# Order of the routing work ahead of the experts' blocks, and how the first block's input is scaled

## The chip, the cores and the metric

The kernel runs on one core of a Trainium2 chip. The metric is the device time of one execution in microseconds, as a median of several runs. The engines of the core are PE (TensorE), DVE (VectorE), ACT (ScalarE), POOL (GpSimd) and SP (SyncE, which issues the DMAs of the weights here). Each engine works off its own instructions in the order in which they stand, and waits at semaphores for the others.

## What is computed

Two transformer blocks over 256 tokens of 1024 channels, all in float32. The change touches the last step of the second block alone, a mixture of 16 experts in 4 groups:

```python
def hier_moe(h, w_rg, b_rg, w_re, b_re, w1, w3, w2):
    t = h.reshape(-1, d)
    lg = (t @ w_rg + b_rg).astype(jnp.float32)
    g_sel = jnp.argmax(lg, axis=-1)
    w_grp = jnp.take_along_axis(jax.nn.softmax(lg, axis=-1), g_sel[:, None], axis=-1)
    le = (t @ w_re + b_re).astype(jnp.float32).reshape(-1, N_GROUPS, EXPERTS_PER_GROUP)
    le_g = jnp.take_along_axis(le, g_sel[:, None, None], axis=1)[:, 0]
    top_v, top_i = lax.top_k(le_g, TOP_K_IN_GROUP)
    w_top = jax.nn.softmax(top_v, axis=-1) * w_grp
    ...
        y = (jax.nn.silu(t @ w1e) * (t @ w3e)) @ w2e
        return acc + ge[:, None] * y, None
```

`h` is the RMS-normed stream, times (1 + scale), plus a shift. The result is gated, added to the stream and normed once more.

## The kernel before

Ahead of the experts, `merge2` makes the stream `h` (tile `res`) in 8 slices of 128 channels. Beside each slice PE also makes the router's logits (L1371) and transposes the slice to token rows (L1376, tiles `xh`, `xl`), and `sumsq` gathers the squares for the norm: ACT squares, DVE or POOL add four slices up, and PE sums them over the channels after the fourth and the eighth slice (L343).

`moe` then runs: `tokens` starts the output's accumulators with the stream (L1733), `route` makes the routing, and 13 blocks of 64 slots follow. A slot is a place for one token. Experts 12 to 15 have a block each (blocks 0 to 3). The other twelve are sorted by how many tokens they have; the fullest get two blocks, the emptiest share one. So the weights of the experts from block 4 on can be loaded only when the sorted order (`order`, tile `idi`) is known: SP reads the twelve numbers one by one (L1753) and issues the DMAs with them. Weights come as tiles of 1 MB (`ew`), six for an expert, 96 in all, into 19 slots of memory. SP's instructions have one order, so a DMA stands behind the reads that are ahead of it.

`route` is a Python generator: each `next(route)` emits one part of it. Before, part one ends with `rk`, the rank of each token in its expert (L1444); part two makes the gates (the softmaxes, L1452 to L1473); part three makes the experts' order, then per expert the ranks and gates in that order, then the list of extra blocks `eji` for experts that overflow (`moe_rest`, normally none).

For a block, `onehots` makes a matrix `Q` from ranks to slots, `norms` and `rows` gather the slots' token rows with it (PE L1586, L1627; ACT scales them into `xs`), `modulated_slots` transposes them into one bank (PE L1641), and DVE multiplies by `a2` and adds the shift over all 8 slices at once (L1644, L1645; tile `xX`). `per_slot` makes the transposed matrix `xPT` and the slots' gates `gs` (PE L1598, L1612). Then `expert_in` (PE L1674) makes both products into `gu`, `expert_act` makes `xa` (ACT tanh, two instructions of DVE: L1683, L1684), `expert_mid` transposes it (L1692, `xaT`), `expert_out` multiplies by the last weight (L1706), DVE and ACT scale and split it (`xY`), and `expert_add` adds it to the accumulators (L1721). The blocks are staggered: out and add of a block run beside the next ones' input.

The order on each engine is set by the tile framework's scheduler, which places instructions by its own timeline; priorities follow the order of the source, and in the changed kernel `issue_after` keeps an instruction behind another.

Of the kernel before, what the change touches and what calls it, by code (L numbers as in the profile page):

```python
# [15 lines left out]
OP = mybir.AluOpType  # L16
# [161 lines left out]
class Build:  # L178
# [118 lines left out]
    def slab(self, name, n):  # L297
# [33 lines left out]
    def sumsq(self, st, x, tiles, k, eng=None, alone=KT):  # L331

        nc = self.nc
        sq = self.R([128, x.shape[1]], "nt")
        nc.scalar.activation(sq, x, AF.Square)
        if k % 4 and k < alone:
            (eng or nc.gpsimd).tensor_tensor(self.sq, self.sq, sq, op=OP.add)
        else:
            self.sq = sq
        if k % 4 == 3 or k >= alone - 1:  # L340
            for i in reversed(range(len(tiles))):
                t0, n = tiles[i]
                nc.tensor.matmul(st[:n, i:i + 1], self.sq[:, t0:t0 + n], self.ones[:, 0:1], start=False,  # L343
                                 stop=k == KT - 1 and i == 0)

    def rstd(self, st, nt, dim, eps):
# [3 lines left out]
        r = self.R([128, 4], "rr")  # L350
        nc.gpsimd.tensor_tensor(r[:, :nt], v[:, :nt], self.mhalf[:, 0:1].to_broadcast([128, nt]), op=OP.pow)
        return r
# [994 lines left out]
    def merge2(self):  # L1347
# [17 lines left out]
        for k in range(KT):  # L1365
# [30 lines left out]
    def route(self):  # L1396
# [18 lines left out]
        def onehot(name, x):  # L1415
# [28 lines left out]
        ranked = nc.vector.scalar_tensor_tensor(self.rk, pc[:, 0:32].rearrange("p (i e) -> p i e", i=2), 1000.0,  # L1444
                                                sel, op0=OP.add, op1=OP.mult)
        self.ranked = ranked.ins
# [31 lines left out]
        tt(F, pn[:, 0:16][:, None, :].to_broadcast([128, 3, 16]), cr, OP.is_gt)  # L1478
        Ff = F.rearrange("p r e -> p (r e)")
# [25 lines left out]
    def order(self, cnt):  # L1505
# [8 lines left out]
        nc.vector.scalar_tensor_tensor(key, cnt, 16.0, self.C("pri12"), op0=OP.mult, op1=OP.add)  # L1514
        t, M = self.R([128, 12, 12], "mx7"), self.R([128, 12, 12], "mx8")
        tt(t, across(key), down(key), OP.is_gt)
# [4 lines left out]
        self.ids = self.T([128, 12], "idi", I32)  # L1521
        nc.vector.tensor_copy(self.ids, ids)
        rgs = self.small([128, 2, 2, 12], "rgs")
        for a in range(2):
# [47 lines left out]
    def equal(self, rk, w):  # L1572
        m = rk.shape[2]
        Q = self.R([128, 2, m * w], "xQ", dt=F32R)
        self.nc.vector.tensor_tensor(Q.rearrange("p i (a s) -> p i a s", a=m),
                                     self.C("iota")[:, None, None, :w].to_broadcast([128, 2, m, w]),
                                     rk[:, :, :, None].to_broadcast([128, 2, m, w]), op=OP.is_equal)
        return Q

    def norms(self, Q):  # L1580

        nc = self.nc
        m = Q.shape[2]
        ps = self.P("r")
        for i in range(2):
# [48 lines left out]

    def modulated_slots(self, xs, b):

# [5 lines left out]
        X = self.R([128, KT, 64], "xX")  # L1642
        wide = lambda x: x[:, :, None].to_broadcast([128, KT, 64])
        nc.vector.tensor_tensor(X, bank, wide(self.a2), op=OP.mult)  # L1644
        nc.vector.tensor_tensor(X, X, wide(self.mod[:, 24:32, 0]), op=OP.add)  # L1645
        return X
# [17 lines left out]
    def expert_in(self, ws, X):  # L1664
# [5 lines left out]
        for k in range(KT):  # L1670
            for b, w in enumerate(ws):
                for j in range(2):
                    p = 64 * j + m * b
                    nc.tensor.matmul(gu[p:p + m], X[:, k, m * b:m * b + m], w[k // 2][:, k % 2, j], start=k == 0,  # L1674
                                     stop=k == KT - 1)
        return gu
# [47 lines left out]
    def tokens(self):  # L1724
# [4 lines left out]
        self.acc = [self.P(t) for t in "gggr"]  # L1729
        for i in range(2):  # L1730
            for j in range(2):
                for x in (self.xh, self.xl):
                    nc.tensor.matmul(self.acc[2 * i + j], idr, x[:, i, j * 512:(j + 1) * 512], start=x is self.xh,  # L1733
                                     stop=False)

    def moe(self):
# [7 lines left out]
        Q = self.onehots(0)  # L1744
        xs = self.rows(Q, self.norms(Q))
        X = self.modulated_slots(xs, 0)
        a = Ys = PT1 = None
        ids, wins, wouts = {}, {}, {}
        for e in range(N + 1):
# [6 lines left out]
            if e == 0:  # L1756
                next(route)
            if e < N:
                PT, g = self.per_slot(Q, e % 2, self.gate_cols(e))
                if e % 2 and e + 1 < N:  # L1760
                    Q = self.onehots(e + 1)
                    xs = self.rows(Q, self.norms(Q))
                if e == 0:
                    X1 = self.modulated_slots(xs, 1)
                gu = self.expert_in([wins[x] for x in self.BLOCKS[e]], X)
                if e == 0:
                    X = X1
            before = a
# [8 lines left out]
            if e == 0:  # L1777
                next(route)
            if e:
# [130 lines left out]
```

## Time and profile before

| what | us |
|---|---|
| median of 3 runs | 1182.49 (1181.82 to 1184.79) |
| the profiled execution | 1179.23 |
| its span, first to last instruction | 1177.4 |
| PE busy | 1130.7 (96% of the span) |
| DVE busy | 717.7 (61%) |
| ACT busy | 521.8 (44%) |
| the stage from the end of `merge2` to the last instruction | about 937 to 1177 |

A page of a profile tells of one execution. Times in rows are microseconds from the first instruction. A row of a timeline is start, duration, engine, line, operation, output<-inputs, form, and count; in brackets stands how long the engine was idle before it and whose result ended that. A float32 matmul shows as two records. In a list of waits stand the waiting engine and line, whom it waited for, and us in total, times, longest. The lines are those of the kernel before; in the changed kernel L1586 is L1609, L1627 is L1650, L1644 is L1668, L1674 is L1701.

### The profile page before, as it was taken

The page shows a single profiled execution, that of the slowest core. Times are in us where ns is not written, and L with a number is a line of the kernel's source. Part 1 is how long each engine was busy: PE and PEld are TensorE (multiplying, and loading weights), DVE is VectorE, ACT ScalarE, POOL GpSimd, SP SyncE. Part 2 cuts the span into 40 slices and gives each one's busy share as a digit, 9 for nine tenths or more (in the row PEclk, how much of TensorE's full clock was granted, in tenths as well). Part 3 has the DMA queues.
Part 4 walks back from the last instruction along what each step waited for, and adds up shares of the span by engine and source line. Part 5 has one row for each costly group of instructions (what it writes and reads, how often), then busy time and mean ns, then how long its engine had stood idle before and what let it go on. Part 6 is the DMA issues. An engine that isn't in the chain of part 4 may idle for free. (4 is left out here: it accounts for less than half of the span.)

```text
span 1177.4 us, 21644 instructions
## 1 busy us (share of the span) xinstructions
PE 1130.7 (96%) x8718; PEld 946.6 (80%) x8718; DVE 717.7 (61%) x1341; ACT 521.8 (44%) x1068; POOL 274.9 (23%) x299
## 2 busy tenths in 40 slices
PE   6999899999999998999999999999999989999995
PEld 6888799799998998999999999988999844433331
DVE  6868964966555588998445654777556554322333
ACT  6556563344543564545444443566543312212222
POOL 3341237101222236615230156011003100000000
PEclk9999999799999998999999999999999999999998
DMA  6433333132576565897545444312757769999993
GB/s 233 147 140 109 108 108 108 37 112 105 207 265 250 181 235 211 319 362 274 207 177 180 146 144 168 121 70 80 288 183 275 287 233 421 412 421 422 421 421 123
DMA packets 37574, 256.42 MB, mean 218 GB/s; under 512 B 4064, under 2 KB 5600, under 8 KB 7136
## 3 DMA queue, kind: packets, MB, share of 16 engines
q1 hardware_dynamic: 35280, 250.85, 56.7%
q10 hardware_dynamic: 2192, 4.17, 1.1%
q8 instruction: 69, 1.13, 0.4%
q14 instruction: 33, 0.27, 0.1%
HBM read 253.96 MB, written 1.05 MB: 217 GB/s over the span
## 5 line engine op out<-in xcount | busy, mean ns | idle before, releaser
L319 DVE TENSOR_TENSOR w<-raw,w 128x1024 fp32r<-128x1024 f32 (+1 forms) x233 | 296.3, 1282 | 146.6 <-ACT w L318 137.2
L318 ACT ACTIVATE w<-raw 128x1024 fp32r<-128x1024 f32 (+1 forms) x233 | 242.9, 1054 | 236.1 <-PE d L314 142.2
L311 PE MATMUL d<-xh,w 128*128 128x256 f32 (+3 forms) x520 | 138.8, 300 | 1.1 <-ACT xh L318 1.1
L312 PE MATMUL d<-xh,w 128*128 128x256 f32 (+3 forms) x520 | 135.5, 293 | 0.0
L311 PEld LDWEIGHTS d<-xh,w 128*128 128x128 f32 (+1 forms) x520 | 100.3, 193 | 7.3 <-issue 2.9
L1674 PE MATMUL d<-ew,xX 128*64 128x512 f32 (+1 forms) x544 | 102.5, 598 | 0.1
L312 PEld LDWEIGHTS d<-xh,w 128*128 128x128 f32 (+1 forms) x520 | 100.3, 193 | 2.5 <-issue 1.6
L314 PE MATMUL d<-xl,w 128*128 128x256 f32 (+3 forms) x520 | 82.5, 292 | 0.0
L311 PE MATMUL d<-lxh,w 128*128 128x256 f32 x288 | 75.3, 297 | 0.9 <-ACT vc L1211 0.9
L312 PE MATMUL d<-lxh,w 128*128 128x256 f32 x288 | 71.5, 284 | 0.0
L314 PEld LDWEIGHTS d<-xl,w 128*128 128x128 f32 (+1 forms) x520 | 69.5, 188 | 2.1 <-issue 1.1
L1674 PEld LDWEIGHTS d<-ew,xX 128*64 128x64 f32 (+1 forms) x544 | 29.7, 124 | 49.3 <-issue 45.4
L311 PE MATMUL d<-n2h,w 128*128 128x256 f32 x256 | 63.9, 286 | 0.8 <-ACT ur L1054 0.8
L312 PE MATMUL d<-n2h,w 128*128 128x256 f32 x256 | 63.1, 284 | 0.0
L311 PEld LDWEIGHTS d<-lxh,w 128*128 128x128 f32 x288 | 54.8, 190 | 2.9 <-issue 1.3
L1132 DVE SCALAR_TENSOR_TENSOR E<-wmod,sc,E 128x512 f32<-128x512 f32 x56 | 54.5, 974 | 3.0 <-ACT E L1130 1.6
L312 PEld LDWEIGHTS d<-lxh,w 128*128 128x128 f32 x288 | 54.9, 191 | 0.8 <-issue 0.3
L1824 POOL TENSOR_TENSOR fst<-fst,mhalf 128x1 f32<-128x1 f32 x2 | 1.1, 540 | 233.1 <-DVE fst L1823 233.1
L1706 PE MATMUL d<-ew,xaT 128*64 128x512 f32 (+1 forms) x272 | 52.9, 599 | 0.0
L311 PEld LDWEIGHTS d<-n2h,w 128*128 128x128 f32 x256 | 49.0, 191 | 2.2 <-ACT ur L1054 1.2
L1056 POOL TENSOR_TENSOR uu<-ur 128x256 f32<-128x256 f32 x32 | 35.0, 1092 | 61.5 <-ACT ur L1054 61.5
L312 PEld LDWEIGHTS d<-n2h,w 128*128 128x128 f32 x256 | 49.0, 192 | 0.3 <-DVE E L1132 0.2
(552 smaller groups left out, 2709.8 us busy)
## 6 DMA issues: line engine op xcount, KB each, us to landing
ew<-we_in SPq DMA_DIRECT2D x96, 1024.0 KB, 12.1
raw<-w_in SPq DMA_DIRECT2D x62, 1024.0 KB, 4.9
wmod<-wmod_in SPq DMA_DIRECT2D x24, 1024.0 KB, 6.7
raw<-wup_in SPq DMA_DIRECT2D x16, 1024.0 KB, 5.1
raw<-wdn_in SPq DMA_DIRECT2D x16, 1024.0 KB, 5.0
raw<-wao_in SPq DMA_DIRECT2D x8, 1024.0 KB, 5.0
raw<-wbg_in SPq DMA_DIRECT2D x4, 1024.0 KB, 4.9
raw<-wbd_in SPq DMA_DIRECT2D x4, 1024.0 KB, 6.0
```

The costliest lines, as they stand in the source:

```text
L311: nc.tensor.matmul(ps, wh[:, k, :m], xh[:, k, ts], start=first and k == 0, stop=False)
L312: nc.tensor.matmul(ps, wl[:, k, :m], xh[:, k, ts], start=False, stop=False)
L314: nc.tensor.matmul(ps, wh[:, k, :m], xl[:, k, ts], start=False, stop=last and k == kts - 1)
L318: nc.scalar.activation(h, src, AF.Copy)
L319: (eng or nc.gpsimd).tensor_tensor(l, src, h.bitcast(F32), op=OP.subtract)
L1056: nc.gpsimd.tensor_tensor(u, r, r, op=OP.mult)
L1132: nc.vector.scalar_tensor_tensor(t, w(k), sc[:, 2 * k:2 * k + 1], t, op0=OP.mult, op1=OP.add)
L1674: nc.tensor.matmul(gu[p:p + m], X[:, k, m * b:m * b + m], w[k // 2][:, k % 2, j], start=k == 0, stop=k == KT - 1)
L1706: nc.tensor.matmul(y[p:p + m], aT[:, c, m * b:m * b + m], w[c // 2][:, c % 2, j * 512:(j + 1) * 512], start=c == 0, stop=c == 3)
L1824: nc.gpsimd.tensor_tensor(st[:, 3:4], st[:, 2:3], self.mhalf, op=OP.pow)
```

## The change

Five edits, all around the routing.

- `sumsq` in `merge2` gets `alone=6`: the sixth, seventh and eighth slices are summed by PE each as they come, and DVE's additions for the last two go. `rstd` writes to its place at once, without a copy.
- In `route` the two products of the ranks over a column block become one, and three matmuls of ones by ones (`busy`) stand ahead of them, two more ahead of `norms`. Their results are overwritten.
- The experts' order is made directly behind the ranks, from a copy of the counts (`cnt`). Gates, and ranks and gates in the new order (`ordered`), stand behind the first block's input; the extra blocks are made beside block 4.
- Block 0's input is scaled and shifted in halves: four slices by DVE, four by ACT.
- The transposed matrix and gates of block 0 and the input of block 1 stand behind the third step of block 0's `expert_in`.

```diff
+    def busy(self, ps, n, after):
+        with self.tc.issue_after(after):
+            for _ in range(n):
+                self.nc.tensor.matmul(ps[:, :128], self.ones, self.ones, start=True, stop=True)
...
-            self.sumsq(st, h, self.REAL, k, nc.vector if k > 3 else nc.gpsimd)
+            self.sumsq(st, h, self.REAL, k, nc.vector if k > 3 else nc.gpsimd, alone=6)
...
-        nc.vector.tensor_copy(r, self.rstd(self.tot, 2, D, EPS)[:, :2])
+        self.rstd(self.tot, 2, D, EPS, r)
...
-        nc.tensor.matmul(pc[:, 0:16], C("trius"), sel[:, 0], start=True, stop=True)
-        nc.tensor.matmul(pc[:, 16:32], C("trius"), sel[:, 1], start=True, stop=False)
+        self.busy(pc, 3, self.begun)
+        nc.tensor.matmul(pc[:, 0:32], C("trius"), sel.rearrange("p i e -> p (i e)"), start=True, stop=False)
         nc.tensor.matmul(pc[:, 16:32], self.ones, sel[:, 0], start=False, stop=True)
...
-        nc.tensor.matmul(pn[:, 0:16], self.ones, sel[:, 1], start=False, stop=True)
+        self.ranking = nc.tensor.matmul(pn[:, 0:16], self.ones, sel[:, 1], start=False, stop=True).ins
+        cnt = R([128, 16], "cnt")
+        nc.vector.tensor_copy(cnt, pn[:, 0:16])
+        self.order(cnt[:, 0:12])
+        yield
...
-        cap = self.order(pn[:, 0:12])
+        cap = self.ordered()
+        yield
...
+        n = KT // 2 if halves else KT
+        wide = lambda x: x[:, :n, None].to_broadcast([128, n, 64])
+        nc.vector.tensor_tensor(X[:, :n], bank[:, :n], wide(self.a2), op=OP.mult)
+        ins = nc.vector.tensor_tensor(X[:, :n], X[:, :n], wide(self.mod[:, 24:32, 0]), op=OP.add)
+        self.shifted = ins.ins
+        for k in range(n, KT):
+            nc.scalar.activation(X[:, k], bank[:, k], AF.Identity, bias=self.sh2(k), scale=self.a2[:, k:k + 1])
...
-        xs = self.rows(Q, self.norms(Q))
-        X = self.modulated_slots(xs, 0)
+        with self.tc.issue_after(self.placed):
+            next(route)
+        xs = self.rows(Q, self.norms(Q, 2))
+        X = self.modulated_slots(xs, 0, True)
+        shifted = self.shifted
...
             if e == 0:
-                next(route)
-            if e < N:
+                gu = self.expert_in([wins[x] for x in self.BLOCKS[e]], X)
+                with self.tc.issue_after(shifted):
+                    with self.tc.issue_after(self.third):
+                        next(route)
+                        PT, g = self.per_slot(Q, 0, self.gate_cols(0))
+                        X = self.modulated_slots(xs, 1)
...
             if e == 0:
-                next(route)
+                with self.tc.issue_after(shifted):
+                    next(route)
+            if e == 4:
+                with self.tc.issue_after(self.shifted):
+                    next(route)
```

How the order moves, at three places. PE, from the last matmul of `tokens` to the first gathered row (`tabs` holds the triangle of ones, `small` the routing's little tiles), before:

```order
L1733 MATMUL r<-xl,idr 128x512
L1441 MATMUL d<-small,tabs_8673 128x16
L1442 MATMUL d<-small,tabs_8673 128x16
L1443 MATMUL d<-small,ones 128x16
L1586 MATMUL r<-small,xQ 128x1 x2
L1627 MATMUL r<-xh,xQ 128x512
```

and after:

```order
L1763 MATMUL r<-xl,idr 128x512
L309 MATMUL d<-ones 128x128 x3
L1449 MATMUL d<-small,tabs_8673 128x32
L1450 MATMUL d<-small,ones 128x16
L1456 MATMUL r<-small,ones 128x16
L1457 MATMUL r<-small,ones 128x16
L309 MATMUL r<-ones 128x128 x2
L1609 MATMUL r<-small,xQ 128x1 x2
L1650 MATMUL r<-xh,xQ 128x512
```

Three products of the ranks became two, and the counts (L1456, L1457; before they stood behind the transposes of block 0's input) and five matmuls of ones came in.

DVE, from the ranks to block 0's input, before (the last row is the first step of `order`'s comparisons):

```order
L1444 SCALAR_TENSOR_TENSOR small<-d,small 128x32
L1575 TENSOR_TENSOR xQ<-tabs_8673,small 128x256 x2
L1588 COPY ns<-r 128x1
L1644 TENSOR_TENSOR xX<-r,a_3943 128x512
L1514 SCALAR_TENSOR_TENSOR small<-r,tabs_8673 128x12
L1645 TENSOR_TENSOR xX<-xX,mod 128x512
L1615 COPY gs<-r 64x1
L1644 TENSOR_TENSOR xX<-r,a_3943 128x512
L1508 TENSOR_TENSOR mx_10931<-small 128x144
```

and after:

```order
L1451 SCALAR_TENSOR_TENSOR small<-d,small 128x32
L1595 TENSOR_TENSOR xQ<-tabs_8673,small 128x256 x2
L1459 COPY small<-r 128x16
L1525 SCALAR_TENSOR_TENSOR small<-small,tabs_8673 128x12
L1611 COPY ns<-r 128x1
L1519 TENSOR_TENSOR mx_10831<-small 128x144
L1520 TENSOR_REDUCE small<-mx_10831 128x12
L1519 TENSOR_TENSOR small<-small,tabs_8673 128x144
L1519 TENSOR_TENSOR mx_10831<-small,tabs_8673 128x144
L1520 TENSOR_REDUCE small<-mx_10831 128x12
L1533 CAST idi<-small 128x12
L1668 TENSOR_TENSOR xX<-r,a_3943 128x256
```

The whole of `order`, down to the numbers that SP reads, moved from behind block 1's input to ahead of block 0's.

DVE beside the step from block 0 to block 1 (the first row scales block 1's input, `xa` is block 0's activation), before:

```order
L1644 TENSOR_TENSOR xX<-r,a_3943 128x512
L1508 TENSOR_TENSOR mx_10931<-small 128x144
L1683 SCALAR_TENSOR_TENSOR xa<-xa,d 64x512
L1645 TENSOR_TENSOR xX<-xX,mod 128x512
L1509 TENSOR_REDUCE small<-mx_10931 128x12
```

and after:

```order
L1668 TENSOR_TENSOR xX<-r,a_3943 128x512
L1539 TENSOR_TENSOR mx_10949<-small 128x144 x2
L1539 TENSOR_TENSOR mx_10953<-small 128x144 x2
L1638 COPY gs<-r 64x1
L1712 SCALAR_TENSOR_TENSOR xa<-xa,d 64x512
L1669 TENSOR_TENSOR xX<-xX,mod 128x512
L1540 TENSOR_REDUCE small<-mx_10949 128x24
```

Four multiplications of 128x144 and a copy now stand between the two halves of block 1's input, where one multiplication stood.

## Rows read from the trace of the kernel before

**Rows 1.** Busy time by stretch: PE, PEld, DVE, ACT, POOL, clock, DMA share, GB/s.
```profile
980.00:1020.00 40.00, 39.46 (x244) 17.35 (x242) 12.03 (x22) 7.54 (x16) 0.00 (x0) 1.00 1.01 415
```
**Rows 2.** What PE waited for from 980 us on: total us, times, longest.
```profile
PE g L1721 <- DVE xY L1714: 5.7, 5, 2.2
PE r L1692 <- DVE xa L1684: 3.7, 4, 1.2
```
**Rows 3.** Timeline of SP: the last issue of a weight tile.
```profile
1134.78 0.33 SPq L1660 DMA_DIRECT2D ew<-we_in  x1
```
**Rows 4.** DMAs of the weight tiles from 880 us on: issue to landing.
```profile
DMA to landing us min/median/max: 4.9/14.1/20.2
```
**Rows 5.** The view of Rows 1 in 5 us steps around the ranks.
```profile
940.00:945.00 5.00, 2.31 (x15) 1.72 (x14) 4.10 (x27) 0.79 (x3) 0.00 (x0) 1.00 1.00 415
945.00:950.00 5.00, 5.00 (x21) 3.50 (x21) 0.66 (x2) 1.68 (x4) 0.00 (x0) 0.66 0.34 144
```
**Rows 6.** Timeline of PE, from the last sum of squares to block 0.
```profile
937.26 0.50 PE L343 MATMUL r<-ones,nt 128*128 128x1 f32 x4
...
942.84 0.39 PE L1441 MATMUL d<-small,tabs 128*128 128x16 f32 x2 [1.86 <-DVE small L1401]
...
944.51 0.58 PE L1586 MATMUL r<-small,xQ 128*128 128x1 f32 x4 [0.83 <-DVE xQ L1575]
...
945.27 0.39 PE L1627 MATMUL r<-xl,xQ 128*128 128x512 f32 x1
945.50 0.56 PE L1627 MATMUL r<-xh,xQ 128*128 128x512 f32 x1
...
948.13 1.34 PE L1641 MATMUL r<-identm,xs 64*128 64x64 f32 x8
...
950.97 6.22 PE L1674 MATMUL d<-ew,xX 128*64 128x512 f32 x26
```
**Rows 7.** Timeline of DVE over the same stretch.
```profile
935.85 0.41 DVE L1380 TENSOR_TENSOR xl<-g,xh 128x256 fp32r<-128x256 f32 x1
...
938.79 0.17 DVE L1407 COPY small<-rr 128x2 f32<-128x2 f32 x1 [0.82 <-POOL rr L351]
...
940.62 0.16 DVE L1405 TENSOR_REDUCE small<-small 128x2 f32<-128x8 f32 x1 [0.31 <-ACT small L1460]
...
949.50 0.69 DVE L1644 TENSOR_TENSOR xX<-r,a 128x512 f32<-128x512 f32 x1 [4.21 <-PE r L1641]
...
950.23 0.69 DVE L1645 TENSOR_TENSOR xX<-xX,mod 128x512 f32<-128x512 f32 x1
```
**Rows 8.** Timeline of ACT ahead of block 0: a large and a small tile.
```profile
936.90 0.38 ACT L1379 ACTIVATE xh<-g 128x256 fp32r<-128x256 f32 x1 [0.27 <-PE g L1376]
...
940.38 0.20 ACT L1460 ACTIVATE small<-small 128x8 f32<-128x8 f32 x1
```
**Rows 9.** Timeline of PE, from the end of block 0 to block 2.
```profile
961.80 6.23 PE L1674 MATMUL d<-ew,xX 128*64 128x512 f32 x28
...
971.25 0.50 PE L1627 MATMUL r<-xh,xQ 128*128 128x512 f32 x1 [0.64 <-DVE ns L1588]
...
973.43 0.71 PE L1641 MATMUL r<-identm,xs 64*128 64x64 f32 x8 [0.60 <-ACT xs L1631]
...
978.48 6.22 PE L1674 MATMUL d<-ew,xX 128*64 128x512 f32 x26
```
**Rows 10.** Timeline of DVE beside blocks 0 and 1.
```profile
959.65 0.69 DVE L1644 TENSOR_TENSOR xX<-r,a 128x512 f32<-128x512 f32 x1 [2.02 <-PE r L1641]
...
960.47 0.67 DVE L1683 SCALAR_TENSOR_TENSOR xa<-xa,d 64x512 f32<-64x512 f32 x1
961.07 0.68 DVE L1645 TENSOR_TENSOR xX<-xX,mod 128x512 f32<-128x512 f32 x1
...
963.96 0.52 DVE L1508 TENSOR_TENSOR mx<-small,mx 128x144 f32<-128x144 f32 x2
```
**Rows 11.** Timeline of PE near the end: the add of the last block but one.
```profile
1159.77 1.22 PE L1721 MATMUL g<-xY,xPT 128*128 128x512 f32 x3 [1.25 <-DVE xY L1714]
```

More of the change, by code (lines that the diff above doesn't have):

```diff
@@ L342, in sumsq, with rstd @@
                 t0, n = tiles[i]
-                nc.tensor.matmul(st[:n, i:i + 1], self.sq[:, t0:t0 + n], self.ones[:, 0:1], start=False,
-                                 stop=k == KT - 1 and i == 0)
-    def rstd(self, st, nt, dim, eps):
+                ins = nc.tensor.matmul(st[:n, i:i + 1], self.sq[:, t0:t0 + n], self.ones[:, 0:1], start=False,
+                                       stop=k == KT - 1 and i == 0)
+            self.summed = ins.ins
+    def rstd(self, st, nt, dim, eps, r=None):
         nc = self.nc
@@ L349, in rstd @@
         nc.vector.tensor_scalar(v[:, :nt], st[:, :nt], 1.0 / dim, eps, op0=OP.mult, op1=OP.add)
-        r = self.R([128, 4], "rr")
+        r = self.R([128, 4], "rr") if r is None else r
         nc.gpsimd.tensor_tensor(r[:, :nt], v[:, :nt], self.mhalf[:, 0:1].to_broadcast([128, nt]), op=OP.pow)
@@ L1440, in route @@
         pc = self.P("d")
-        nc.tensor.matmul(pc[:, 0:16], C("trius"), sel[:, 0], start=True, stop=True)
-        nc.tensor.matmul(pc[:, 16:32], C("trius"), sel[:, 1], start=True, stop=False)
+        self.busy(pc, 3, self.begun)
+        nc.tensor.matmul(pc[:, 0:32], C("trius"), sel.rearrange("p i e -> p (i e)"), start=True, stop=False)
         nc.tensor.matmul(pc[:, 16:32], self.ones, sel[:, 0], start=False, stop=True)
-        ranked = nc.vector.scalar_tensor_tensor(self.rk, pc[:, 0:32].rearrange("p (i e) -> p i e", i=2), 1000.0,
-                                                sel, op0=OP.add, op1=OP.mult)
-        self.ranked = ranked.ins
+        nc.vector.scalar_tensor_tensor(self.rk, pc[:, 0:32].rearrange("p (i e) -> p i e", i=2), 1000.0,
+                                       sel, op0=OP.add, op1=OP.mult)
         self.r2 = r
@@ L1474, in route @@
         yield
-        cap = self.order(pn[:, 0:12])
+        cap = self.ordered()
+        yield
         F, cr = R([128, 3, 16], "Fc"), self.small([128, 3, 16], "cr3")
         tt(cr, C("r64").rearrange("p (r e) -> p r e", r=3), cap[:, None, :].to_broadcast([128, 3, 16]), OP.add)
-        tt(F, pn[:, 0:16][:, None, :].to_broadcast([128, 3, 16]), cr, OP.is_gt)
+        tt(F, cnt[:, None, :].to_broadcast([128, 3, 16]), cr, OP.is_gt)
         Ff = F.rearrange("p r e -> p (r e)")
@@ L1514, in order @@
         nc.vector.scalar_tensor_tensor(key, cnt, 16.0, self.C("pri12"), op0=OP.mult, op1=OP.add)
-        t, M = self.R([128, 12, 12], "mx7"), self.R([128, 12, 12], "mx8")
+        t, M = self.R([128, 12, 12], "mx7"), self.small([128, 12, 12], "mof")
         tt(t, across(key), down(key), OP.is_gt)
@@ L1522, in order, with ordered @@
         nc.vector.tensor_copy(self.ids, ids)
+        self.place, self.mof = place, M
+    def ordered(self):
+        nc = self.nc
+        tt = lambda o, a, b, op: nc.vector.tensor_tensor(o, a, b, op=op)
+        red = lambda o, a: nc.vector.tensor_reduce(o, a, axis=AX.X, op=OP.add)
+        across = lambda x: x[:, None, :].to_broadcast([128, 12, 12])
+        place, M = self.place, self.mof
         rgs = self.small([128, 2, 2, 12], "rgs")
@@ L1574, in equal, with norms @@
         Q = self.R([128, 2, m * w], "xQ", dt=F32R)
-        self.nc.vector.tensor_tensor(Q.rearrange("p i (a s) -> p i a s", a=m),
-                                     self.C("iota")[:, None, None, :w].to_broadcast([128, 2, m, w]),
-                                     rk[:, :, :, None].to_broadcast([128, 2, m, w]), op=OP.is_equal)
+        ins = self.nc.vector.tensor_tensor(Q.rearrange("p i (a s) -> p i a s", a=m),
+                                           self.C("iota")[:, None, None, :w].to_broadcast([128, 2, m, w]),
+                                           rk[:, :, :, None].to_broadcast([128, 2, m, w]), op=OP.is_equal)
+        self.placed = ins.ins
         return Q
-    def norms(self, Q):
+    def norms(self, Q, busy=0):
         nc = self.nc
@@ L1584, in norms @@
         ps = self.P("r")
+        if busy:
+            self.busy(ps, busy, self.ranking)
         for i in range(2):
@@ L1633, in rows, with modulated_slots @@
         return xs
-    def modulated_slots(self, xs, b):
+    def modulated_slots(self, xs, b, halves=False):
         nc = self.nc
@@ L1642, in modulated_slots @@
         X = self.R([128, KT, 64], "xX")
-        wide = lambda x: x[:, :, None].to_broadcast([128, KT, 64])
-        nc.vector.tensor_tensor(X, bank, wide(self.a2), op=OP.mult)
-        nc.vector.tensor_tensor(X, X, wide(self.mod[:, 24:32, 0]), op=OP.add)
+        n = KT // 2 if halves else KT
[5 more added lines that the diff above has]
+            nc.scalar.activation(X[:, k], bank[:, k], AF.Identity, bias=self.sh2(k), scale=self.a2[:, k:k + 1])
         return X
@@ L1673, in expert_in @@
                     p = 64 * j + m * b
-                    nc.tensor.matmul(gu[p:p + m], X[:, k, m * b:m * b + m], w[k // 2][:, k % 2, j], start=k == 0,
-                                     stop=k == KT - 1)
+                    ins = nc.tensor.matmul(gu[p:p + m], X[:, k, m * b:m * b + m], w[k // 2][:, k % 2, j],
+                                           start=k == 0, stop=k == KT - 1)
+                    if k == 2:
+                        self.third = ins.ins
         return gu
@@ L1729, in tokens @@
         self.acc = [self.P(t) for t in "gggr"]
[L1730 to L1734, printed above, removed]
+        with self.tc.issue_after(self.summed):
+            for i in range(2):
+                for j in range(2):
+                    for x in (self.xh, self.xl):
+                        ins = nc.tensor.matmul(self.acc[2 * i + j], idr, x[:, i, j * 512:(j + 1) * 512],
+                                               start=x is self.xh, stop=False)
+        self.begun = ins.ins
     def moe(self):
@@ L1756, in moe @@
             if e == 0:
-                next(route)
-            if e < N:
+                gu = self.expert_in([wins[x] for x in self.BLOCKS[e]], X)
[4 more added lines that the diff above has]
+                        X = self.modulated_slots(xs, 1)
+            elif e < N:
                 PT, g = self.per_slot(Q, e % 2, self.gate_cols(e))
```

4 lines of the change are left out of this document (removed).

## Prediction

> **What bounds the kernel now.** I read the view by stretch first, for the expert blocks. Between 980 and 1020 us PE is busy for 39.46 of 40.00 us at clock 1.00 [rows 1]; the DMA engines are as full there, at a share of 1.01, so the second question is whether PE ever waits for a weight. It doesn't: the two largest entries in the list of its waits from 980 us on are the adds waiting for `xY` (5.7 us in 5 waits) and the transposes waiting for `xa` (3.7 in 4), both for DVE [rows 2]. The last weight tile is issued at 1134.78 [rows 3], and no tile took more than 20.2 us to land [rows 4], so it is there by about 1155.0; PE reaches the add of the last block but one at 1159.77 [rows 11], and only then the rest of the last products. Weights have some 5 us in hand at the tightest place. From this two things follow. Earlier weights are worth nothing by themselves; and if PE starts a block earlier by less than about 5 us, the end comes earlier by as much. So the question is how early blocks 0, 1 and 2 start.
>
> The timelines of PE and DVE between 935 and 980 us answer it. There PE is not full: 2.31 of 5 us from 940 to 945 [rows 5]. It waits 1.86 us for DVE's chain to the ranks and 0.83 for `xQ` [rows 6], then its granted clock is 0.66 on the mean of the next 5 us [rows 5], that is, part of these at the lower level.
>
> **The change part by part.** All sums are made against the profiled execution, 1179.23 us with a span of 1177.4 (1.8 lie around it); the median of the runs, 1182.49, is 3.3 us longer, and I take the difference over unchanged.
>
> Sums of squares. Two more groups of channel sums come to a full PE. Four records took 0.50 us [rows 6], and their spacing is less, so each group costs between 0.2 and 0.5; I take 0.36, together −0.72. In exchange DVE loses an addition of four slices; the nearest row is an operation of 128x256 at 0.41 [rows 7], and with the order of `xh` and `xl` behind it I take 0.55 back. The copy that goes (0.17 [rows 7]) comes on top. Net about 0, bounds −0.5 to +0.5.
>
> Gates out of the chain to the ranks. In it DVE waits 0.31 us for ACT's exponential at 940.62 [rows 7]; that wait and a small instruction go: +0.35. The product of ranks in one goes from three pairs of records to two: at most 0.39, the duration of such a pair [rows 6]; I take 0.23, the spacing of two records, from 945.27 to 945.50 [rows 6]. The counts and the matmuls of ones stand in time in which PE waited (1.86 and 0.83 [rows 6]), so they cost nothing unless they last longer than that: three before the ranks and, behind them, two counts and two of ones, each of these below 0.39 by the counts' kin in [rows 6], some 0.9 us together against about 1 us in which DVE makes `rk` and `xQ`. At worst +0.2 of delay.
>
> The clock. Two gathers with the same shape follow each other by 0.23 us at 945.27 [rows 6]; from 945.50 six of them take until 948.13, 2.63 us, where 6 x 0.23 makes 1.4. Ahead of the fall stood the two waits of PE. With the five matmuls of ones and the counts in them most of that idle time is filled, and I let the fall go: +1.2. The bounds are 0 (the clock falls all the same) and +1.7 (the transposes, 1.34 us against 0.71 for the same eight [rows 6, 9], are shorter too, as far as ACT's scaling of `xs` does not hold them). A page speaks against taking this as sure. Trainium skill, "TensorE: Matmul & The Clock Gate", section "Part 1: The HAM clock gate": the watch over PE's activity runs freely, so the same kernel showed different numbers of matmuls at the lower clock from run to run. By that rule filling the waits makes the fall rarer, not impossible, and the 1.2 us would be 0 in some executions; no run before shows more than one execution's clock, so it can't be weighed further here.
>
> Block 0's input. From the first multiplication at 949.50 to block 0 at 950.97 lie 1.47 us: two operations of 0.69 each [rows 7]. In halves DVE makes two of 128x256; at the row of that size, 0.41 [rows 7], that is 0.8: +0.6. ACT's four instructions of 128x64 lie between its 0.20 for 128x8 and 0.38 for 128x256 [rows 8], so 0.8 to 1.5 together; they wait for DVE's multiplication since they read the same bank, and PE needs their first slice behind four of eight steps of block 0, half of 6 to 7 us later [rows 6]. Hidden; if ACT had to go first, it would cost its 0.8 to 1.5 back. `order`'s seven small DVE instructions stand ahead of this multiplication, at 0.2 to 0.3 us each; DVE idles for 4.21 us there [rows 7], less 1.2 if the clock holds. Hidden too. Block 0 starts 0 + 0.35 + 0.23 + 1.2 + 0.6 = 2.4 us earlier.
>
> From block 0 to block 1. The transposed matrix of block 0 moves from the wait for DVE into block 0, and the matrix products for the gates out of it: about equal. But DVE's four multiplications for the new order (two took 0.52 [rows 10], so 1.0) and a copy stand between the two steps of block 1's input, where one of about 0.25 stood: from the multiplication at 959.65 to block 1 at 961.80 [rows 9, 10] it took 2.15 us, now 2.15 + 0.75 = 2.9. PE waits for that: −0.75, so block 1 starts 1.65 earlier. Behind DVE's four also waits `xa` of block 0 (960.47 [rows 10]), which PE uses only beside block 1.
>
> From block 1 to block 2, 16.68 us [rows 9]. `norms` for blocks 2 and 3 now stands ahead of block 1, in the wait that was just lengthened: 0.58 for its records [rows 6], of which I take 0.5. The gathers' wait of 0.64 for it goes, and the wait of 0.60 for `xs` [rows 9] with it, as ACT has the norms long before. +1.75: block 2 starts 3.4 us earlier.
>
> The later blocks. The list of extra blocks, about ten us of DVE, stood beside block 1 and now stands beside blocks 4 and 5, where DVE is busy 12.03 of 40 us [rows 1]; ahead of it in the queue wait `xY` and an `xa` at most, with 2 to 3 us of room by the order's place. I take 0, with −2 as the bound. SP reads eight numbers ahead of a weight that it issued before without them, and four more; weights have 5 us in hand, 0. In the last block but one the add waits 1.25 us for `xY` [rows 11]; in the new order more products stand ahead of it: +0.5. The sum is 2.4 − 0.75 + 1.75 + 0.5 = 3.9 us.
>
> **The rivals.** One: the clock falls all the same, inside the gathers or, shifted, inside block 0, where it would cost more, since products at the lower level take twice as long, as the gathers did; or it did not fall in the executions that were timed. Then 1.2 us or up to 1.7 are missing: 3.9 − 1.5 = 2.4, 1180.1 us. For it speaks that the idle time ahead of the ranks stays in part, as DVE's chain is the same; against it that PE's waits get filled on both sides of the ranks.
>
> Two, on the other side: covers are lost in blocks 5 to 12. The scheduler has written the order anew there, at some nine places: the transposes of `xa`, the adds and the products stand differently around one another. Before, where such a cover lacked, PE waited 3.7 / 4 = 0.9 us for `xa` and 5.7 / 5 = 1.1 for `xY` [rows 2]. A block whose chain through ACT and DVE is no longer covered costs 1 us each time. Four such places take the 3.9 us away; from five on the kernel is slower, and all nine would give 1182.5 - 3.9 + 9 = 1187.6. For it speaks that nothing in the change looks after these places; against it that PE's products there are many and equal, and only few orders leave no cover.
>
> Three: the early order has a worth of its own, the change's plain sense. It would need a weight that was late before. No entry of [rows 2] is one. If the wait for `xY` falls away in full beside it, 5.7 us, the time would be near 1175.
>
> **How the numbers follow.** The forecast, 1182.49 − 3.9, is 1178.6, put at 1178.5 us: 0.48. The clock's rival, 1180: 0.20. The lost covers 0.24: 0.14 of it costs two to four places and lands between 1180.5 and 1183, 0.10 costs many and lands above 1186, slower by more than the bound below. The larger gain, 1175.5 or less: 0.08. About 0.3%, 3.5 us, is what a measurement of this kernel can tell from no change; faster than that means below 1178.9. The forecast lies just at that bound, so of its 0.48 I count 0.34 as faster and 0.14 as the same, with the clock's rival on the side of the same but for 0.03: faster 0.34 + 0.03 + 0.08 = 0.45, slower 0.10, the same 0.14 + 0.17 + 0.14 = 0.45. The sum of the bounds, −0.5 to +0.5 at the sums of squares and −2 at the extra list, widens both ends: 1175.5 to 1182.5 leaves out 0.06 below and some 0.13 above.
>
> **What would show it.** In the changed kernel's view by stretch the clock from 943 to 948 us is 1.00; if it shows 0.66 again, the first rival holds. Block 0's first product starts near 948.5, block 1's near 960.1, block 2's near 975.0. The numbers that SP reads are there by about 946.5. Between the two steps of block 1's input lie 2.9 us from start to block, and in the list of PE's waits from 975 us on stands no weight, and for `xa` and `xY` no more than 9.4 us together. If that sum is larger by 4 us or more, the second rival holds. If block 2 starts 3.4 us earlier and the end does not, a cover or a weight took the gain, and I would be wrong about the room of 5 us.

## The result and the profile after

Timed beside each other, seven runs each, the changed kernel takes 1175.19 us (median; 1173.71 to 1179.19) and the kernel before 1181.82: a ratio of 0.9948, interval 0.9935 to 0.9961. Two later series of the same kernel gave 0.9957 (0.9940 to 0.9975) and 0.9951 (0.9932 to 0.9970). On the 1182.49 us that the forecast started from, 0.9948 makes 1176.3; the forecast was 1178.5, range 1175.5 to 1182.5. The way was right, the size was 3.9 us where 4.6 to 7.7 were measured. The median itself, 1175.19, lies 0.3 us below the range; the kernel before was at 1181.82 beside it, 0.7 below the time that the forecast started from.

The first profile of the changed kernel happened to be its slowest execution: 1179.19 us, span 1177.0, only 0.4 us shorter than in the profile of before. So first its view by stretch, with columns as in [rows 1]:

```profile
940.00:945.00 5.00, 4.79 (x35) 3.80 (x34) 3.46 (x17) 0.73 (x2) 0.71 (x1) 1.00 0.98 367
945.00:950.00 5.00, 4.71 (x31) 3.60 (x30) 3.09 (x13) 1.68 (x4) 0.00 (x0) 1.00 0.78 328
950.00:955.00 5.00, 4.18 (x12) 1.31 (x14) 2.71 (x20) 1.48 (x6) 0.00 (x0) 0.66 0.02 5
...
980.00:1020.00 40.00, 39.46 (x240) 17.04 (x237) 12.46 (x22) 8.20 (x17) 0.00 (x0) 1.00 0.98 392
```

Against [rows 5], PE is busy 4.79 of 5 us around the ranks where it was 2.31 (part of that is a shift of the whole execution, shown below: in the 5 us of before that lie as far behind the fifth slice, 938.05 to 943.05, it was 3.14), and the clock is 1.00 up to block 0. But the 0.66 hasn't gone: in this execution it stands one stretch later, in block 0. The expert blocks are as full as in [rows 1]. Now PE's timeline, from the router's products of the fifth slice (the last place that the change does not reach) to block 2:

```profile
929.25 0.52 PE L1378 MATMUL r<-tabs,res 128*128 128x20 f32 x4
...
938.83 0.62 PE L1378 MATMUL r<-tabs,res 128*128 128x20 f32 x4 [0.58 <-DVE res L1376]
...
944.60 0.41 PE L1449 MATMUL d<-small,tabs 128*128 128x32 f32 x2 [0.21 <-DVE small L1408]
...
946.49 0.47 PE L1650 MATMUL r<-xh,xQ 128*128 128x512 f32 x1
...
950.82 6.21 PE L1701 MATMUL d<-ew,xX 128*64 128x512 f32 x20 [0.98 <-DVE xX L1669]
...
963.64 6.22 PE L1701 MATMUL d<-ew,xX 128*64 128x512 f32 x26 [0.27 <-DVE xX L1669]
...
979.15 6.22 PE L1701 MATMUL d<-ew,xX 128*64 128x512 f32 x26
```

In before the fifth slice's products start at 927.30. So this execution was already 1.95 us late where nothing had been changed, and absolute times mislead. From here on I count every step from that place. The same distances in four profiles, worked out as differences of starts:

| from the fifth slice's router products to | before | after, first | after, again |
|---|---|---|---|
| the last slice's router products | 8.69 | 9.58 | 9.58 |
| the ranks' products | 15.54 | 15.35 | 15.35 |
| the first gathered row | 17.65 | 17.24 | 17.24 |
| block 0 | 23.68 | 21.57 | 21.57 |
| block 1 | 34.51 | 34.39 | 32.70 |
| block 2 | 51.18 | 49.90 | 48.21 |
| the end | 250.11 | 247.73 | 245.86 |

A third profile of after, `after_third` below, repeats the last column up to block 2. Up to block 2 these distances agree to some hundredths wherever the clock is the same; where it falls, they jump. The end is less sharp: 245.86 and 245.59 in the second and third profile of after. That still makes traces far sharper than times here: one kernel's runs spread over 4 to 8 us.

What PE waits for from 980 us on is, in its two large rows, what it was in [rows 2], and no weight is among it:

```profile
PE g L1750 <- DVE xY L1743: 5.7, 5, 2.2
PE r L1721 <- DVE xa L1713: 3.7, 4, 1.2
```

### The profile page after: what moved, and what is told of

Same layout as the page of the kernel before. It is cut to its first block, busy times and chain, and to the rows that moved or that the text cites. A ratio compares the mean times of both kernels' runs of the same rounds, so it can differ in the third digit from the quotient of the medians.

```text
span 1177.0 us, 21685 instructions
## 1 busy us (share of the span) xinstructions
PE 1132.2 (96%) x8734; PEld 949.8 (81%) x8734; DVE 717.0 (61%) x1339; ACT 523.2 (44%) x1072; POOL 276.7 (24%) x299
```

## The experiments

Each changes the changed kernel (once the one before) in one place, mostly, and is read by the same distances.

**The two kernels again.** No edit.

> The kernel before once more, for the spread of one kernel and a second look at the clock. Theory A (the granted clock falls in the gathers of block 0's rows because PE has paused twice ahead of them, so it falls in every execution): ratio 1.000 +- 0.002, clock about 0.66 again between the ranks and block 0, and 51.2 us from the fifth slice's router products (L1371) to block 2's first product, as in the profile of before (927.30 to 978.48). Theory B (where the clock falls is chance from one execution to the next): the same ratio, but the fall stands elsewhere or is missing; without it the distance is about 49.9 us, with it inside block 0 about 51.7.

Measured: 1182.62 us, ratio 0.9998 (0.9982 to 1.0014). The fall of the clock came again, at the same place, 18.46 us from the fifth slice's router products, which I call the mark from here on (18.27 in the first profile), but it lasted 10.2 us in place of 3.4. One more of 3.4 us came 49.2 us from the mark, between block 1 and block 2. The view by stretch:

```profile
945.00:950.00 5.00, 4.16 (x19) 3.03 (x19) 1.71 (x9) 0.84 (x2) 0.00 (x0) 0.77 0.76 321
950.00:955.00 5.00, 5.00 (x26) 3.19 (x28) 1.46 (x3) 1.23 (x3) 0.00 (x0) 0.50 0.02 3
955.00:960.00 5.00, 5.00 (x20) 1.57 (x18) 0.00 (x0) 0.00 (x0) 0.00 (x0) 0.70 0.38 123
```

From 950 to 955 PE is busy all the time and the clock is 0.50, the lower of its two levels. Block 1 and the products ahead of block 2, here and then in the first profile:

```profile
966.39 6.23 PE L1674 MATMUL d<-ew,xX 128*64 128x512 f32 x28
...
978.75 5.18 PE L1706 MATMUL d<-ew,xaT 128*64 128x512 f32 x16
```
```profile
974.07 3.65 PE L1706 MATMUL d<-ew,xaT 128*64 128x512 f32 x16
```

Block 1 starts at 37.11 from the mark, 2.6 us later than in the first profile: that is what the longer fall cost. Block 2 starts at 55.41, 4.2 us later: the other 1.6 are the second fall's, in which the same sixteen records take 5.18 us and not 3.65. So theory A holds in the place of the fall and not in its size: in before the fall is there in both profiles, at one place, and its length varies.

> The changed kernel once more. In its first profile the clock stayed at the full level up to block 0 and fell inside block 0; from the fifth slice's router products (L1378) to block 2 it took 49.9 us (929.25 to 979.15) and 247.8 to the end, before 51.2 and 250.1. Theory A (filling PE's waits holds the clock in most executions, the first profile was an exception): no fall near block 0, 48.3 us to block 2 and about 246.2 to the end; ratio 0.994 to 0.997. Theory B (the fall is chance): again a fall somewhere between the ranks and block 1, about 49.9 us; ratio the same.

Measured: 1176.41 us, ratio 0.9957. No fall: block 1 starts 1.69 us earlier than in the first profile, and with it all that follows. So in the changed kernel the fall inside block 0 comes in some executions and not in others; the third profile of after has none either.

```profile
928.08 0.52 PE L1378 MATMUL r<-tabs,res 128*128 128x20 f32 x4
...
949.65 4.51 PE L1701 MATMUL d<-ew,xX 128*64 128x512 f32 x20 [0.98 <-DVE xX L1669]
...
960.78 6.22 PE L1701 MATMUL d<-ew,xX 128*64 128x512 f32 x26 [0.27 <-DVE xX L1669]
```

**Without the matmuls of ones.**

```diff
-        self.busy(pc, 3, self.begun)
...
-        xs = self.rows(Q, self.norms(Q, 2))
+        xs = self.rows(Q, self.norms(Q))
```

> The changed kernel without its five matmuls of ones, all else as it was. Theory A (they hold the clock): the clock falls in the gathers or in block 0, block 2 starts 1.2 to 1.7 us later than without a fall, median about 1.2 us over the changed kernel's, ratio to before 0.996 to 0.998. Theory B (they are worth nothing, the fall is chance): median within 0.6 us of the changed kernel's. In both the ranks' products start no earlier, since DVE's chain sets them.

Measured: 1178.50 us, 0.9974 (0.9960 to 0.9988), 2.1 us above the changed kernel timed beside it, though the two intervals (0.9940 to 0.9975 there) still overlap. PE's timeline:

```profile
943.41 0.41 PE L1448 MATMUL d<-small,tabs 128*128 128x32 f32 x2 [0.88 <-DVE small L1408]
...
944.87 0.58 PE L1608 MATMUL r<-small,xQ 128*128 128x1 f32 x4 [0.38 <-DVE xQ L1594]
...
946.22 0.63 PE L1649 MATMUL r<-xl,xQ 128*128 128x512 f32 x1
```

The pauses are open again (0.88 and 0.38), and the gathers last 0.63 each where [rows 6] has 0.39 at the full level: the fall is back at its old place, 17.8 from the mark. Block 0 starts 22.72 from the mark, 1.15 later.

**The matmuls of ones alone, in the kernel before.** The same five, at the same two places, and `busy` itself.

> The kernel before with the five matmuls of ones alone: three ahead of the ranks' products, two ahead of the first norms. Theory A (PE's pauses around the ranks let the clock fall, the matmuls of ones hold it): clock 1.00 between the ranks and block 0, block 0's first product about 22.6 us behind the fifth slice's router products in place of 23.68, median 1 to 2.5 us below the kernel before, ratio 0.998 to 0.999, mean granted clock of the runs near 0.985 in place of 0.982. Rival (the clock is held in the changed kernel by its shorter chain, not by these matmuls): clock and median as before, ratio 1.000 +- 0.001.

Measured: 1181.19 us, 0.9996 (0.9982 to 1.0009). Theory A fell in this form.

```profile
942.37 0.40 PE L1448 MATMUL d<-small,tabs 128*128 128x16 f32 x2 [1.20 <-DVE small L1407]
...
943.95 0.61 PE L1595 MATMUL r<-small,xQ 128*128 128x1 f32 x4 [0.20 <-DVE xQ L1582]
944.42 0.55 PE L1636 MATMUL r<-xh,xQ 128*128 128x512 f32 x1
944.77 0.63 PE L1636 MATMUL r<-xl,xQ 128*128 128x512 f32 x1
```

Here 1.20 us of the first pause stay open, and the gathers are slow from the second one on. Block 0 starts 23.92 from the mark, 0.24 later than in the first profile of before, and a second fall of 3.4 us stands in block 1. In the changed kernel only 0.21 of that pause stays. An edit that the list of the change leaves out has a part in it: `tokens` issues its products behind the last sum of squares. The last of them starts 14.08 from the mark where it was 13.28, so they end 0.8 later, and the ranks' products start 0.2 sooner (15.35 for 15.54). That edit was not tried by itself. PE's pauses between the token products and the first gather, and the fall: 2.69 us in before, 1.40 with the ones alone, 1.26 in the changed kernel without them, each with the fall in or at the gathers; 0.2 to 0.3 in the changed kernel and all its variants with the ones, ten profiles, none with it there. Neither part did it alone, in one profile each.

**More matmuls of ones**, four in the last pause ahead of block 0.

```diff
-                gu = self.expert_in([wins[x] for x in self.BLOCKS[e]], X)
+                gu = self.expert_in([wins[x] for x in self.BLOCKS[e]], X, 4)
...
+        if busy:
+            self.busy(gu, busy, self.turned)
```

> The changed kernel with four more matmuls of ones ahead of block 0's first product, in PE's last pause there (0.98 us, for the shift of block 0's input); they write into the bank that block 0's first product overwrites. Theory A (that pause is what lets the clock still fall inside block 0 in some executions, as in the first profile of the changed kernel): no fall near block 0, fewer slow executions: median 1 us or so below the changed kernel's, ratio to before 0.993 to 0.995, highest run nearer to the median. Theory B (the fall is chance): spread and median as in the changed kernel, 0.994 to 0.997. If the four outlast the pause, block 0 starts up to 0.3 us later in both.

Measured: 1174.92 us, 0.9945 (0.9925 to 0.9965), highest run 1179.15; no fall near block 0 in the profile, and distances as in the changed kernel (21.62, 32.75, 48.26). Inconclusive: two of the changed kernel's three profiles have no fall there either.

**Block 0's input whole.**

```diff
-        X = self.modulated_slots(xs, 0, True)
+        X = self.modulated_slots(xs, 0)
```

> The changed kernel with block 0's input scaled and shifted by DVE alone, over all eight slices. By the sum on record (two halves at 0.41 in place of two wholes at 0.69) block 0's first product starts 1.4 us behind the start of DVE's multiplication in place of about 0.9, so blocks and end come 0.5 to 0.6 us later than in the changed kernel: about 0.0005 in the ratio. Rival (PE waits for ACT's half or for the transposes anyway, so the halves give nothing): block 0 no later against the gathers, and the end within 0.2 us.

Measured: 1177.76 us, 0.9967 (0.9952 to 0.9982). The rows of DVE, then of PE:

```profile
951.12 0.69 DVE L1668 TENSOR_TENSOR xX<-r,a 128x512 f32<-128x512 f32 x1 [1.28 <-PE r L1664]
951.84 0.69 DVE L1669 TENSOR_TENSOR xX<-xX,mod 128x512 f32<-128x512 f32 x1
```
```profile
952.59 2.83 PE L1701 MATMUL d<-ew,xX 128*64 128x512 f32 x6 [1.51 <-DVE xX L1669]
```

PE waits 1.51 us ahead of block 0 where the halves leave 0.98; block 0 starts 22.12 from the mark and not 21.57: the halves are worth 0.55. In this profile the clock fell in block 0 and again in block 1, and the last add stood elsewhere, so the rest of the time is not the halves'.

**The sums as before.**

```diff
-            self.sumsq(st, h, self.REAL, k, nc.vector if k > 3 else nc.gpsimd, alone=6)
+            self.sumsq(st, h, self.REAL, k, nc.vector if k > 3 else nc.gpsimd)
```

> The changed kernel with the squares summed as before, after the fourth and the eighth slice only. Distances count from the fifth slice's router products. In the changed kernel the last slice's products start 9.58 us and the ranks' 15.35 us behind that, before 8.69 and 15.54. Theory A (the sum on record: two more groups cost PE some 0.8, and DVE's addition and the order of xh and xl give back less): last slice at 8.69 again, ranks at 15.1 +- 0.1, so blocks and end up to 0.3 us EARLIER than in the changed kernel. Rival (the early sums pay): ranks at 15.4 to 15.6, blocks later by as much. In both below what the runs' times can tell; the trace decides.

Measured: 1175.26 us, 0.9940 (0.9921 to 0.9958). The last slice is back at 8.69, the ranks' products start at 14.87 and block 0 at 21.09 (943.72 and 949.94 from 928.85):

```profile
943.72 0.41 PE L1449 MATMUL d<-small,tabs 128*128 128x32 f32 x2 [0.27 <-DVE small L1408]
...
949.94 1.51 PE L1701 MATMUL d<-ew,xX 128*64 128x512 f32 x6 [0.98 <-DVE xX L1669]
```

So the early sums cost 0.48 us: theory A held, with more than was expected of it. The end comes at 244.21, 1.65 earlier than in the changed kernel; the other 1.1 to 1.2 us come from the last adds, which the scheduler has placed otherwise here.

**The new order's multiplications behind block 1's input.**

```diff
             if e == 0:
-                with self.tc.issue_after(shifted):
+                with self.tc.issue_after(self.shifted):
                     next(route)
```

> The changed kernel with the ranks and gates in the new order (the four multiplications of 128x144) held behind the second step of block 1's input. Theory A (they stand on the path, as the sum on record has it with 0.75): from block 0 to block 1 10.1 to 10.4 us where the changed kernel takes 11.13 without a fall of the clock, from block 1 to block 2 the same 15.5, so block 2 0.75 to 1.0 earlier. Rival (PE waits there for something else, such as the gates): 11.1 again. What the later blocks make of it hangs on the order the scheduler writes there: up to 0.75 us either way.

Measured: 1174.80 us, 0.9943 (0.9923 to 0.9964). DVE, first in the changed kernel's second profile, then here:

```profile
957.91 0.69 DVE L1668 TENSOR_TENSOR xX<-r,a 128x512 f32<-128x512 f32 x1 [6.01 <-PE r L1664]
958.52 0.95 DVE L1539 TENSOR_TENSOR mx<-small 128x144 f32<-128x144 f32 x4
...
960.05 0.68 DVE L1669 TENSOR_TENSOR xX<-xX,mod 128x512 f32<-128x512 f32 x1
```
```profile
958.10 0.69 DVE L1668 TENSOR_TENSOR xX<-r,a 128x512 f32<-128x512 f32 x1 [6.00 <-PE r L1664]
958.71 0.14 DVE L1638 COPY gs<-r 64x1 f32<-64x1 f32 x1
...
959.37 0.68 DVE L1669 TENSOR_TENSOR xX<-xX,mod 128x512 f32<-128x512 f32 x1
```

From one step of block 1's input to the other it is 2.14 us with the four, 1.27 without. Block 0 to block 1 takes 10.28 in place of 11.13, block 2 starts 0.76 earlier. The four stand on the path. The end comes at 244.59; most of what block 2 gained is lost by block 12, and as in `sums_late` the last adds stand better.

**The experts' order late.** `order` moves from behind the counts to ahead of `ordered`; SP's numbers then come about 16 us later.

```diff
-        self.order(cnt[:, 0:12])
         yield
...
+        self.order(cnt[:, 0:12])
         cap = self.ordered()
```

> The changed kernel with the experts' order made behind block 1's input, with its ranks and gates, as before; the rest of the change stays. SP's numbers then come some 15 us later. Theory A (no weight was late, so early numbers are worth nothing; the sum on record has 0): PE waits for no weight, block 4 and the end no later than in the changed kernel, and from block 0 to block 1 10.2 to 10.7 in place of 11.1, since one multiplication of 128x144 stands there and not four. Rival (the early order is what the change gains by): PE waits for weights from block 4 on, end 2 us or more later against block 2.

Measured: 1176.32 us, 0.9953 (0.9935 to 0.9971). PE's waits from 975 us on:

```profile
PE g L1750 <- DVE xY L1743: 6.3, 6, 2.2
PE r L1721 <- DVE xa L1713: 3.6, 4, 1.2
```

No weight among them. Block 1 starts at 10.47 behind block 0, block 2 at 46.78 from the mark, 1.43 earlier than in the changed kernel. Of that 0.66 lie ahead of block 1, where DVE has less to do, and 0.80 between block 1 and block 2 (14.71 for 15.51). The second part is PE's order. Block 1's end in the changed kernel's second profile, then all of block 1 here:

```profile
969.01 1.93 PE L1701 MATMUL d<-ew,xX 128*64 128x512 f32 x6
```
```profile
959.80 6.23 PE L1701 MATMUL d<-ew,xX 128*64 128x512 f32 x28
...
968.01 1.08 PE L1701 MATMUL d<-ew,xX 128*64 128x512 f32 x4
```

The eight gathers stand between these records in both. A step of `expert_in` is two products, four records. Here the gathers stand behind the 28th record, so between two steps; in the changed kernel behind the 26th, inside a step, and the 32 records take 0.8 us more.

The end comes at 246.04, not earlier. What block 2 gained went on the way: 0.70 up to block 12, 0.91 behind it, with one more wait for `xY` (6.3 in 6) and last adds that stand less well. So no worth of the early order shows, within the 1 us or so that the scheduler's places move the end; it costs DVE time ahead of block 1.

**Both costly edits back** (the diffs of the sums and of the multiplications together).

> The changed kernel with both edits that cost time there taken back: squares summed after the fourth and eighth slice only, and ranks and gates in the new order held behind the second step of block 1's input. If the two add up as they did alone (0.48 at the ranks, 0.85 at block 1), block 0 starts 21.1 us behind the fifth slice's router products, block 1 31.4, block 2 46.9 to 47.0, the end comes 243 to 244 behind it in place of 245.9, median 1172.5 to 1174.5. Rival (the scheduler's order of the later blocks takes it back, as it did behind block 5 in other runs): block 2 as said, the end at 245 or later.

Measured: block 0 at 21.09, block 1 at 31.37, block 2 at 46.96: up to there the two add up, 1.25 us less than in the changed kernel. The end at 243.80 is 2.1 us earlier, but each alone already came to 244.21 and 244.59: about 1.2 us of it are the last adds' places, which all three share. The time says less: 1175.14 us, 0.9953 (0.9935 to 0.9971), between 1172.07 and 1178.39.

**The same with four more matmuls of ones ahead of block 0**, beside the changed kernel on one chip.

> The changed kernel with the two costly edits taken back and four more matmuls of ones ahead of block 0's first product. In the trace block 2 should start 46.9 to 47.0 us behind the fifth slice's router products, as with the two taken back alone. Theory (the spread of the runs from there on comes from falls of the clock in PE's last pause before block 0): mean granted clock of the runs above 0.986, median 1172.5 to 1174, ratio 0.992 to 0.994. Rival (falls elsewhere make the spread): mean clock 0.985, median 1174.5 to 1176, ratio 0.9945 to 0.9965.

> The changed kernel again, on the same chip as the version beside it. Median 1175 to 1176.5, ratio 0.9945 to 0.9965, mean granted clock 0.985 to 0.987; from the fifth slice's router products to block 2 48.2 us if the clock holds, 49.9 if it falls inside block 0. The version beside it is better if its median lies 1.5 us or more below.

Measured: 1175.12 us, 0.9933 (0.9917 to 0.9949), against 1177.03 and 0.9951 (0.9932 to 0.9970). The six runs lie between 1174.48 and 1176.71 at a mean clock of 0.986, those beside them between 1174.81 and 1180.35 at 0.985, with a median above the 1175 to 1176.5 that was expected. The ratio is the lowest of all, and the median 1.9 us below that of the changed kernel, but the intervals overlap. Its own profile had a fall all the same, at block 1's start: block 2 at 48.69. The falls don't all come from the pause ahead of block 0.

## Why the prediction came out as it did

The sum on record, 3.9 us, against the second profile of after, 4.25 us over the first of before:

**Up to the gathers** it had +0.58 and a net of 0 for the sums. Measured 0.41: the chain to the ranks gave 0.89, 0.31 more than summed, and the sums took 0.48. The step that was mis-sized most is the net of the sums; −0.5 was its bound. PE's two groups took 0.89 (8.69 to 9.58), not 0.72, and DVE gave back less than 0.55.

**From the gathers to block 0** it had 1.2 for the clock and 0.6 for the halves. Measured 1.70 (6.03 less 4.33), of which 0.55 are the halves and 1.15 the clock. Right, and in this pair of profiles with the right cause: with the matmuls of ones and a shorter pause together the clock held at the gathers, with either alone it fell.

**Block 0 to block 1** had −0.75 for the wait and 0 for the rest. From block 1's transposes to block 1 it now takes 3.62 us where it was 2.90, −0.72; right, and `order_behind` shows the four multiplications as its cause. Block 0 itself, up to those transposes, got 0.42 shorter (7.93 to 7.51), which "about equal" did not have.

**Block 1 to block 2** had +1.75, measured 1.16 (16.67 to 15.51). The waits of [rows 9] went, 1.24 together. The 0.5 for `norms` did not show: the 32 records of block 1 take 6.15 + 1.86 us (26 and 6, all eight gathers between) where they took 6.15 + 1.07 (28 and 4, four gathers between), and that eats it. `ids_behind` settles what costs it: the same eight gathers behind the 28th record leave 6.16 + 1.01. In `both_back` they stand behind the 30th, again inside a step, and the 32 take 8.0 as well. So in these four orders the 0.8 us go with the broken step, not with the number of gathers; the sum had no term for where they stand. Why PE loses by it was not tried.

**The later blocks** had +0.5, measured 1.28. From block 2 to block 12 the new order is 0.51 us shorter: the way to block 5 is 0.17 longer, to block 6 0.53 shorter, and it stays about there. Block 12 to the end brings the rest, 0.77, beside the last add but one:

```profile
1157.07 0.73 PE L1750 MATMUL g<-xY,xPT 128*128 128x512 f32 x2 [1.24 <-DVE xY L1743]
1157.73 1.07 PE L1735 MATMUL d<-ew,xaT 128*32 128x512 f32 x8
1158.73 0.50 PE L1750 MATMUL g<-xY,xPT 128*128 128x512 f32 x1
```

The wait of [rows 11] is still there at 1.24, but four more records of the last products stand ahead of it and eight between the adds. In `sums_late` those eight stood ahead of it too, and the wait shrank to 0.38:

```profile
1157.33 1.22 PE L1750 MATMUL g<-xY,xPT 128*128 128x512 f32 x3 [0.38 <-DVE xY L1743]
```

So rival two's mechanism is real, places are lost, but more were won. That a term of 0.5 came out at 1.28 is luck of the scheduler's order: nothing in the change looks after it, and `sums_late`, `order_behind` and `both_back` moved the end by another 1.1 to 1.2 us there.

The terms were off by −0.17, −0.10, +0.45, −0.59 and +0.78. That 3.9 lies so near to 4.25 is in part their cancelling.

**What the sum did not have** is the rest up to the measured 5.1 to 6.1 us (0.9957 to 0.9948 of 1182). The prediction took the clock from one execution and put its bound at +1.7; in the second profile of before the fall lasted three times as long and cost 2.6 us more, and a second fall 1.6. The mean over both profiles of before from the mark to the end is 252.3, over the three of after 246.4, 5.9 apart. The granted clock of the timed runs points the same way: on the mean 0.982 over 27 runs of before, 0.987 and 0.985 over the first two series of after (7 each), 0.983 without the ones. But it is a mean over the whole execution, and the lower level varies in unchanged parts too: between 205 and 245 us it lasts 10.2 to 17.1 us in these profiles. So it fits that the other 1.5 us or so come from executions of before in which the clock fell longer or once more; two profiles do not show it.

Rival one was right in a way, too: the changed kernel's first profile had the fall inside block 0, and it cost 1.69 there. From the gathers on the lower level lasted 3.4 and 10.2 us in two profiles of one kernel, and in block 0 3.4 and 0 in two of the other. The Trainium skill, "TensorE: Matmul & The Clock Gate", section "Part 1: The HAM clock gate", says of a kernel's start that the watch runs freely and the number of slow matmuls varies from run to run; these profiles agree with that for the middle of a kernel.

Rival three held nothing: PE waited for no weight, with the early numbers or without. In the weight loads (PEld) of `expert_in` the pauses that a DMA ended are 2.5 us in 6 either way, and none of them is in PE's own list.

The signs on record came out where the clock did not fall: counted from the mark, block 2 was due at 47.7 and came at 48.21, the step in block 1's input takes 2.87 us for 2.9, and the waits for `xa` and `xY` are 9.4 together.

## What to carry to other kernels

Where one engine sets the end and its clock can fall, look at two or three traces of the same kernel before pricing the fall, and fill the pauses ahead of it with something harmless only together with what shortens them. Count distances from the last place that the change does not touch; here, up to block 2, they agreed to hundredths where times spread over several us. Of an instruction that is "moved early because it is short", ask whose two steps it now stands between: four of 0.24 us cost 0.85. And look where foreign products fall among a block's: inside a step they cost 0.8 us more here than between two steps.

## What the runs showed that was not expected

The fall of the clock begins at one place in all profiles that pause ahead of the gathers (17.8 to 18.5 us from the mark, four profiles of three kernels) but lasts 3.4 us in three of them and 10.2 in one, although PE was busy for all of 950 to 955 there. In the ten profiles without that pause three had a fall later, two at the start of block 0 (one of these a second one in block 1) and one at the start of block 1, and what decides it was not found.
